# A hybrid mixer layer on one core: the first branch's projection as seven block products, and one late scan head fewer

## The chip, the core and the metric

One core of a Trainium2 chip runs the whole layer. The metric is device time in microseconds of one execution; lower is better. The core has TensorE (PE, matmuls, whose weight loads the profile calls PEld), VectorE (DVE), ScalarE (ACT), GpSimd (POOL) and SyncE (SP). All transfers that matter here are issued from SP's one queue, in its order.

## The reference

```python
px = hx @ w_in + b_in                      # hx: normed, modulated x, 2048 tokens x 1024
u = c_a * x_a
conv = dwconv3(u, w_conv, b_conv)          # along rows of 64 tokens
y_a = b_a * conv * silu(z_a)               # first branch
h = mLSTM forward + backward, 8 heads, chunkwise
y_b = sigmoid(o) * headnorm(h) * silu(z_b) # second branch
merged = sigmoid(g_a) * (y_a @ w_pa) + sigmoid(g_b) * (y_b @ w_pb)
out = rmsnorm(x + gate * (merged @ w_out + b_out))
```

The projections w_pa, w_pb and w_out are 1024 x 1024; w_in has about 11 such blocks of columns. All data is float32.

## The kernel before

**Precision.** A float32 operand is split into a high part (a cast on ACT to the fast format, `split`, L178) and a low part (a subtraction on DVE, L179). A product is three passes: high x high, high x low, low x high. In the trace `wh` and `wl` are the parts of a weight tile, and `x` names both parts of an operand in the 28 slots of the pool xp.

**Halves and stages.** The 2048 tokens are two halves of 1024. The stages run in this order: input products of half 0; of half 1; then four branch stages, each one projection of one half: w_pa of half 1, w_pb of half 1, w_pa of half 0, w_pb of half 0; then the output product with the final norm.

**Two forms of product.** `pair` (matmuls at L427) multiplies two blocks of 128 output columns and both 512-token column blocks of a half in seven block products in place of eight. Product o (0 to 6) takes operand o of `Operands`, a sum or difference of blocks that `combine` wrote to DRAM ahead of time, and weights that `Stream.make` sums on POOL (four sums a pair, L360). A pair is 7 x 4 x 3 = 84 matmuls of 128x512. After the products DVE and ACT add the bank sums together (s1, u2, u3, and `added` at L926). `slab` (matmuls at L474) is the plain form: one block of 128 columns, 8 x 3 matmuls for each of the two token blocks. Before the change the input and output products use pairs, and all four branch stages use slabs on operands loaded by `Branch`.

**Side work.** The state scans, token transposes, gates and preparation of operands are generators that are advanced between matmuls. `run(dense, rate, urate)` takes one step from the queue `later` for every 1/rate matmuls and one from `urgent` for every 1/urate; `flush` runs what is left. PE's order is the order of the code; the other engines' orders come from a scheduler, apart from instructions under `pin`.

**The scan.** The mLSTM runs in chunks of 128 tokens, 8 per head and half. One chunk is 8 steps. It updates the state (PE L658, then DVE L662), takes the scores of the next chunk (PE L834), applies the weights (ACT wt L832, DVE pt L836 and qw L839), multiplies four times into the one PSUM bank pn (L891, L892), divides on DVE (den, rd, L897 to L900) and normalises (ACT hf L904, DVE hb L905). Bank pn is free again after hb. `state_scan` is a shorter form that only carries the state; it too updates through a bank pn. For half 0 the scan of the first EARLY heads runs under the input products of half 1 and the rest, the late heads, under the branch stages; late heads recompute masks on ACT (L816) and POOL (L820). Each finished head of half 0 is loaded and split as an operand of the last branch stage (`yb.fetch`).

## Time and profile before

| | us |
|---|---|
| median of 3 runs | 2660.72 |
| lowest, highest | 2659.01, 2660.84 |
| profiled execution | 2660.47 |
| its span | 2658.7 |
| input products of half 1 end, branch stages begin | 2076.5 |
| last branch stage ends, output begins | 2484.5 |

A row of the profile that groups instructions reads: line, engine, operation, output<-input, shape, count | busy us, mean ns of one | idle time of that engine just before them, and what ended it. A row of a window of time reads: start:end, length, then the busy time of PE, PEld, DVE, ACT and POOL with their counts, the granted PE clock (1 is full), the busy share of the DMA engines, and GB/s. A row of the timeline reads: start, length, engine, line, operation, in square brackets how long the engine had been idle and what ended it. A row of the waits reads: engine, its output, its line <- who was waited for: total us, times, longest.

### The profile page before, as it was taken

What the parts mean: (1) busy time and instruction counts of PE and PEld (TensorE: products, weight loads), DVE (VectorE), ACT (ScalarE), POOL (GpSimd) and SP (SyncE); (2) the same over time, 40 slices, a digit from 0 to 9 for tenths busy, and PEclk for the clock granted to TensorE, in tenths of its full rate; (3) what the DMA queues carried; (4) which work ended last, traced back from release to release, by engine and by line L of the source; (5) the groups of instructions that cost most, each with busy time, mean ns of one, the idle gap of its engine ahead of it and who ended that gap; (6) DMA issues with size and microseconds to landing.
All of it is one profiled execution on the core that took longest, in us unless ns stands there. A gap on an engine that the chain in (4) does not pass through costs nothing.

```text
span 2658.7 us, 38177 instructions
## 1 busy us (share of the span) xinstructions
PE 2594.5 (98%) x12807; PEld 2166.7 (81%) x12807; DVE 1722.6 (65%) x3119; ACT 1099.0 (41%) x2269; POOL 1123.8 (42%) x1322
## 2 busy tenths in 40 slices
PE   8999999999999999999999999999999999999998
PEld 7788887888878787877887888888888888888777
DVE  6643237687776777478578577667666656554597
ACT  5433344333333335344443444344444544442233
POOL 1221223233345553235555555565555124422674
PEclk9999999999999999999999999999999999999999
DMA  8333344655734457435644653653566978768542
GB/s 231 101 101 106 106 139 131 211 167 179 232 118 123 139 145 236 118 100 159 195 142 130 201 160 120 195 174 128 154 195 201 301 219 273 253 194 288 195 159 96
DMA packets 373217, 452.99 MB, mean 170 GB/s; under 512 B 24428, under 2 KB 273948, under 8 KB 373020
## 3 DMA queue, kind: packets, MB, share of 16 engines
q1 hardware_dynamic: 372784, 450.46, 54.4%
q8 instruction: 102, 1.67, 0.3%
q14 instruction: 95, 0.78, 0.1%
q10 hardware_dynamic: 236, 0.08, 0.0%
HBM read 319.42 MB, written 131.03 MB: 169 GB/s over the span
## 4 chain that ended last, share of the span: by engine, by line
PE 48%; DVE 3%; DMA 2%; issue 1%; POOL 1%; ACT 0%; SPq 0%; DVEq 0%; POOLq 0%; ACTq 0%
PE pd L427 29%; PE pd L474 11%; PE pn L891 2%; PE pn L892 2%; PE pa L834 1%; PE pu L658 1%; DMA mgd<-t2k 1%; DVE wl L179 1%; PE pa L849 1%; PE pn L658 0%; PE pa L669 0%; DVE xt L1596 0%; DVE xt L1605 0%; DMA x<-wod 0%; DVE cv L999 0%
## 5 line engine op out<-in xcount | busy, mean ns | idle before, releaser
L427 PE MATMUL pd<-x,wh 128*128 128x512 f32 x5320 | 1695.9, 397 | 15.9 <-DVE xt L1605 8.5
L427 PEld LDWEIGHTS pd<-x,wh 128*128 128x128 f32 x5320 | 985.1, 189 | 209.9 <-issue 19.4
L427 PE MATMUL pd<-x,wl 128*128 128x512 f32 x2660 | 1057.3, 397 | 0.0
L427 PEld LDWEIGHTS pd<-x,wl 128*128 128x128 f32 x2660 | 501.8, 189 | 99.3 <-issue 0.2
L178 ACT CAST wh<-sw 128x512 fp32r<-128x512 f32 x382 | 237.0, 620 | 492.9 <-PE pd L427 409.0
L179 DVE TENSOR_TENSOR wl<-sw,wh 128x512 fp32r<-128x512 f32 x382 | 303.2, 795 | 182.0 <-ACT wh L178 177.1
L178 ACT CAST wh<-wr 128x512 fp32r<-128x512 f32 x350 | 216.6, 619 | 375.3 <-PE pd L427 269.9
L360 POOL TENSOR_TENSOR sw<-wr,sw 128x512 f32<-128x512 f32 x95 | 136.1, 1433 | 432.6 <-DVE wl L179 345.2
L179 DVE TENSOR_TENSOR wl<-wr,wh 128x512 fp32r<-128x512 f32 x350 | 289.7, 828 | 42.5 <-ACT wh L178 39.1
L474 PE MATMUL pd<-x,wh 128*128 128x512 f32 x896 | 281.7, 396 | 0.0
L360 POOL TENSOR_TENSOR sw<-wr 128x512 f32<-128x512 f32 x95 | 130.9, 1378 | 236.9 <-DVE wl L179 236.0
L653 POOL TENSOR_SCALAR vw<-tk,wk 128x129 f32<-128x129 f32 x205 | 161.9, 794 | 120.2 <-PE pn L658 109.7
L474 PEld LDWEIGHTS pd<-x,wh 128*128 128x128 f32 x896 | 166.3, 188 | 32.1
L474 PE MATMUL pd<-x,wl 128*128 128x512 f32 x448 | 173.4, 397 | 0.0
L186 POOL TENSOR_SCALAR ssq<-ssq 128x1 f32<-128x1 f32 x128 | 37.2, 291 | 293.7 <-ACT hf L906 289.8
L926 DVE TENSOR_TENSOR t2k<-pd,u 128x512 f32<-128x512 f32 x168 | 115.5, 688 | 59.8 <-PE pd L427 59.1
L360 POOL TENSOR_TENSOR sw<-sw,wr 128x512 f32<-128x512 f32 x94 | 132.4, 1408 | 47.9 <-DVE wl L179 37.4
L904 ACT ACTIVATE hf<-pn,rd 128x128 f32<-128x128 f32 x128 | 47.0, 367 | 246.9 <-DVE rd L900 222.4
L360 POOL TENSOR_TENSOR sw<-wr,wr 128x512 f32<-128x512 f32 x94 | 132.2, 1406 | 20.2 <-DVE wl L179 10.8
L820 POOL TENSOR_SCALAR_AFFINE_SELECT mw<-mw 128x256 f32<-128x256 f32 x128 | 61.7, 503 | 119.5 <-DMA mw<-mwd 89.1
L891 PE MATMUL pn<-tk,pt 128*128 128x129 f32 x512 | 98.8, 275 | 5.0 <-DVE hb L905 5.0
L891 PEld LDWEIGHTS pn<-tk,pt 128*128 128x128 f32 x512 | 86.8, 190 | 16.2 <-issue 5.8
(259 smaller groups left out, 3317.5 us busy)
## 6 DMA issues: line engine op xcount, KB each, us to landing
wr<-in_w_in_dram SPq DMA_DIRECT2D x176, 512.0 KB, 4.1
tk<-tokd SPq DMA_DIRECT2D x64, 386.0 KB, 3.6
mw<-mwd SPq DMA_DIRECT2D x44, 512.0 KB, 5.3
qkd<-t2k SPq DMA_DIRECT2D x64, 256.0 KB, 2.9
qk<-qkd SPq DMA_DIRECT2D x64, 256.0 KB, 3.8
tk<-tokd SPq DMA_DIRECT2D x48, 257.0 KB, 2.9
tokd<-t2k SPq DMA_DIRECT2D x32, 258.0 KB, 2.9
x<-in_w_ada_dram SPq DMA_DIRECT2D x16, 512.0 KB, 6.4
```

The lines of the kernel that those rows point to most:

```text
L178: a = nc.scalar.copy(hi, raw)
L179: b = (eng or nc.vector).tensor_tensor(lo, raw, hi.bitcast(F32), op=OP.subtract)
L186: nc.gpsimd.tensor_scalar(dst, ss, 1.0 / n, EPS, op0=OP.mult, op1=OP.add)
L360: nc.gpsimd.tensor_tensor(s, a, b, op=op)
L427: nc.tensor.matmul(ps[b], op[wi][:, kk, :], xs.at(o, xi, kk), start=(fresh and kk + pi == 0), stop=(o == last[b] and kk == 3 and pi == 2), ...
L474: nc.tensor.matmul(pss[j], ops[k // 4][wi][:, k % 4, :], y(xi, k, j), start=(k + pi == 0), stop=(k == NK - 1 and pi == 2))
L653: pin(nc.gpsimd.tensor_scalar(vw, tk[:, VT], wk, None, op0=OP.mult))
L820: pin(nc.gpsimd.affine_select(mws[m][:, :, 0, d, :], mws[m][:, :, 0, d, :], pattern=[[0, 2], [s, P]], base=0, channel_multiplier=-s, compa ...
L891: nc.tensor.matmul(pn[:, d, :], pt[:, d, :], tk[:, VT], start=True, stop=False)
L892: nc.tensor.matmul(pn[:, d, :], qw[:, d, :], cur if d == carried else tk[:, ST], start=False, stop=True)
L904: nc.scalar.activation(hf, pn[:, 0, 0:P], AF.Copy, scale=rd[:, 0:1])
L926: nc.vector.tensor_tensor(t, ps, add, op=OP.add)
```

## The change

The first branch's projection is computed in pairs for both halves, by a new class `Gated`. Its operands come from `yad`, which is now laid out in blocks, and `combine` makes the four differences it needs once the last input pair of the first branch (B3) is through: for half 0 with the big tiles it had, for half 1 (`tile` None) with four 512-wide tiles of the pool cv at a time. The half-0 projection now runs straight after half 0's own input products, ahead of half 1's; its result waits in `mad`, which now has a buffer for each half. The order of stages becomes: input half 0, w_pa half 0, input half 1, w_pa half 1, w_pb half 1, w_pb half 0, output. EARLY goes from 3 to 4, so four heads are late where five were: under w_pa half 1 (rate 0.22) and w_pb half 1 (rate 0.55) in place of three branch stages at 0.305. `arriving` loads and splits the operands of w_pb half 1 during the last pair of w_pa half 1. No flush has a step of the scans left in either version. PE has 11200 rows for 11296.

```diff
-    def combine(src, tile):
+    def combine(src, tile=None):
...
-            if kk < 4:
+            if kk < 4 and tile is None:
+                bs[kk] = [vslot() for _ in range(4)]
+                for n, t in enumerate(bs[kk]):
+                    ld.dma_start(t, src[n, :, kk, :])
+            elif kk < 4:
...
-    yad = scratch("yad", [NK, P, T])
+    yad = scratch("yad", [8, P, 4, NB])
...
-    mad = dp.tile([NK, P, T], F32, name="mad")
+    mad = scratch("mad", [NK, P, T])
...
-                ld.dma_start(yad[half][n, :, S2[j]], v)
+                ld.dma_start(yad[half][2 * (n // 4) + j, :, n % 4, :], v)
...
+    class Gated:
+        def __init__(self, half):
+            self.half = half
+            self.tiles = [(2 * p + i, j) for p in range(4) for i, j in ((0, 0), (1, 1), (1, 0), (0, 1))]
+            self.s = deque()
+        def load(self):
+            if self.tiles:
+                n, j = self.tiles.pop(0)
+                s = vslot()
+                ld.dma_start(s, sad[self.half][n, :, S2[j]])
+                self.s.append(s)
+        def begin(self):
+            self.st = Stream((w_pa, 2 * p * P, True) for p in range(4))
+            self.st.begin()
+            self.y = Operands()
+            self.y.load(yad[self.half], range(7))
+            for _ in range(3):
+                self.load()
+        def pairs(self):
+            for p in range(4):
+                def fin(i, j, ps, add):
+                    s = self.s.popleft()
+                    nc.vector.scalar_tensor_tensor(s, s, 1.0, added(ps, add), op0=OP.add, op1=OP.mult)
+                    ld.dma_start(mad[self.half][2 * p + i, :, S2[j]], s)
+                    self.load()
+                yield pair(self.st, self.y, fin)
...
-        run(pair(st, xA, fin), 0.235, 0.5)
+        run(pair(st, xA, fin), 0.212, 0.5)
+        if w == "B3":
+            urgent.append(combine(yad[0], big))
+    flush(urgent)
+    pa = Gated(0)
+    pa.begin()
+    for dense in pa.pairs():
+        run(dense, 0.212, 0.5)
...
-    EARLY = 3
+    EARLY = 4
...
-        run(pair(st, xB, fin), 0.8 if w in ("q0", "o0", "z0") else 0.34, 0.5)
+        run(pair(st, xB, fin), 0.8 if w in ("q0", "o0", "z0") else 0.358, 0.5)
...
+        if w == "B3":
+            urgent.append(combine(yad[1]))
...
-    run(branch(w_pa, ya, PaEnd, 1), RATE, URATE)
...
-    run(branch(w_pb, yb, PbEnd, 1), RATE, URATE)
...
+    pa = Gated(1)
+    pa.begin()
+    ya = Branch(0, lambda k: ybd[1][k], ())
+    def arriving():
+        yield from gap(1)
+        fs = [ya.fetch(k, 1) for k in range(NK)]
+        for o in range(6):
+            yield from gap(12)
+            for k in (2 * o, 2 * o + 1):
+                if o < 4:
+                    next(fs[k])
+            for k in (2 * o - 4, 2 * o - 3):
+                if o > 1:
+                    next(fs[k], None)
+    for p, dense in enumerate(pa.pairs()):
+        if p == 3:
+            urgent.append(arriving())
+        run(dense, 0.22, 1.0)
...
-    run(branch(w_pa, ya, PaEnd, 0), RATE, 0.5)
+    run(branch(w_pb, ya, PbEnd, 1), 0.55, 0.5)
```

In the new file pairs are at L440, slabs at L487, state updates at L671 and L675, den, rd and hb at L910 to L918, `added` at L939, Gated's product at L1081, pt and qw at L849 and L852.

**First place: DVE at the change from the first branch to the second, half 1.** In the kernel before, ahead of and at the start of the second branch (the weight splits wl of its first blocks, scan instructions, the end product L1502 of the first branch):

```order
L897 SCALAR_TENSOR_TENSOR den_22007<-pn_21992,em_129 128x2
L898 TENSOR_TENSOR den_22007<-pn_21992,den_22007 128x2
L900 RECIPROCAL rd_22010<-den_22007 128x2
L905 SCALAR_TENSOR_TENSOR hb_21812<-pn_21992,rd_22010,hf_22012 128x128
L1502 SCALAR_TENSOR_TENSOR t2k_21946<-t2k_21946,pd_21948 128x512
L179 TENSOR_TENSOR wl_22040<-wr_22027,wh_22039 128x512
L662 SCALAR_TENSOR_TENSOR cst_22070<-cst_21964,dec_10588,pu_22071 128x129
```

In the changed kernel, at the same place, the last rows ahead of den_23077, the first division term whose pn is computed in the second branch (x_5739 and x_5741 are low parts of its operands 6 and 7):

```order
L1081 SCALAR_TENSOR_TENSOR cv_22768<-cv_22768,t2k_23003 128x512
L939 TENSOR_TENSOR t2k_23023<-pd_22917,u_22819 128x512
L179 TENSOR_TENSOR wl_23036<-wr_23027,wh_23035 128x512
L1081 SCALAR_TENSOR_TENSOR cv_22884<-cv_22884,t2k_23023 128x512
L179 TENSOR_TENSOR wl_23040<-wr_23033,wh_23039 128x512
L849 SCALAR_TENSOR_TENSOR pt_22990<-pa_22988,wt_22985 128x256
L852 SCALAR_TENSOR_TENSOR qw_22992<-qk_22749,mw_22751 128x256
L179 TENSOR_TENSOR wl_23046<-wr_23033,wh_23045 128x512
L179 TENSOR_TENSOR x_5739_22921<-x_5739_22921,x_5738_22920 128x1024
L179 TENSOR_TENSOR x_5741_22924<-x_5741_22924,x_5740_22923 128x1024
L910 SCALAR_TENSOR_TENSOR den_23077<-pn_23064,em_129 128x2
```

The end work of a pair and the splits of the new operands now stand ahead of a chunk's division, where one product and one weight split stood.

**Second place: DVE at the end of half 0's input products.** In the kernel before, while half 1's operands are loaded (x names their low parts, L662 is a state update):

```order
L179 TENSOR_TENSOR x_2211_9550<-x_2211_9550,x_2209_9548 128x1024
L662 SCALAR_TENSOR_TENSOR tk_9358<-tk_9358,dec_1466,pn_9473 128x129
L441 TENSOR_TENSOR u_9481<-pd_9461,u_9428 128x512
L662 SCALAR_TENSOR_TENSOR cst_9488<-tk_9358,dec_1466,pn_9489 128x129
L179 TENSOR_TENSOR x_2214_9553<-x_2214_9553,x_2212_9551 128x1024
L179 TENSOR_TENSOR wl_9627<-wr_9622,wh_9626 128x512
L926 TENSOR_TENSOR t2k_9502<-pd_9483,u_9481 128x512
L179 TENSOR_TENSOR x_2215_9554<-x_2215_9554,x_2213_9552 128x1024
L179 TENSOR_TENSOR x_2218_9557<-x_2218_9557,x_2216_9555 128x1024
```

In the changed kernel, while the operands of w_pa half 0 are loaded, at about the same operands:

```order
L179 TENSOR_TENSOR x_2153_9418<-x_2153_9418,x_2151_9416 128x1024
L675 SCALAR_TENSOR_TENSOR tk_9233<-tk_9233,dec_1467,pn_9348 128x129
L179 TENSOR_TENSOR wl_9488<-wr_9407,wh_9487 128x512
L939 TENSOR_TENSOR t2k_9354<-pd_9332,u_9330 128x512
L179 TENSOR_TENSOR wl_9498<-sw_9495,wh_9497 128x512
L179 TENSOR_TENSOR x_2156_9421<-x_2156_9421,x_2154_9419 128x1024
L675 SCALAR_TENSOR_TENSOR cst_9366<-tk_9233,dec_1467,pn_9367 128x129
L939 TENSOR_TENSOR t2k_9377<-pd_9358,u_9330 128x512
L763 COPY tk_9285<-cst_9287 128x129
L179 TENSOR_TENSOR x_2157_9422<-x_2157_9422,x_2155_9420 128x1024
L179 TENSOR_TENSOR wl_9502<-wr_9409,wh_9501 128x512
L675 SCALAR_TENSOR_TENSOR tk_9285<-tk_9285,dec_1467,pn_9397 128x129
```

State updates now go on between the operand splits to the last of them; before, they ended in the middle of the load.

**Third place: PE at the start of the last branch stage (w_pb half 0).** In the kernel before, the last transposes of the scan (L849) and the last matmuls of the stage ahead (bank pd_24317), up to the new stage's first:

```order
L849 MATMUL pa_24336<-ident,hb_23850 128x128 x4
L474 MATMUL pd_24317<-x_5650_22823,wh_24146 128x512
L474 MATMUL pd_24317<-x_5651_22824,wh_24146 128x512
L474 MATMUL pd_24317<-x_5650_22823,wl_24147 128x512
L474 MATMUL pd_24317<-x_5680_22957,wh_24146 128x512
L474 MATMUL pd_24317<-x_5681_22958,wh_24146 128x512
L474 MATMUL pd_24317<-x_5680_22957,wl_24147 128x512
L474 MATMUL pd_24399<-x_5767_23306,wh_24371 128x512
```

In the changed kernel (transposes at L862, the stage ahead in bank pd_24606):

```order
L487 MATMUL pd_24606<-x_5740_22923,wh_24327 128x512
L487 MATMUL pd_24606<-x_5741_22924,wh_24327 128x512
L487 MATMUL pd_24606<-x_5740_22923,wl_24328 128x512
L862 MATMUL pa_24648<-ident,hb_24285 128x128 x4
L487 MATMUL pd_24706<-x_5774_23061,wh_24678 128x512
```

The transposes of the last head stood six matmuls ahead of the new stage and now stand at its first.

34 lines of the change are left out of this document (13 added, 21 removed).

## The prediction

> **What bounds the kernel now.** I read the page's engine table first, then busy time by stage, then what TensorE (PE) waits for in each stage, then the distance between its matmuls.
>
> ```profile
> span 2658.7 us, 38177 instructions
> PE 2594.5 (98%) x12807; PEld 2166.7 (81%) x12807; DVE 1722.6 (65%) x3119; ACT 1099.0 (41%) x2269; POOL 1123.8 (42%) x1322
> core 0: us, PE busy (x) PEld busy (x) DVE busy (x) ACT busy (x) POOL busy (x), PEclk, DMA share, GB/s
> 553.00:1042.00 489.00, 476.96 (x2157) 391.25 (x2157) 361.96 (x552) 188.65 (x292) 212.87 (x189) 0.99 0.53 162
> 1042.00:2076.50 1034.50, 1020.21 (x5150) 854.42 (x5150) 707.28 (x1473) 454.67 (x1006) 537.00 (x682) 1.00 0.54 163
> 2076.50:2485.20 408.70, 408.70 (x2050) 345.43 (x2049) 211.78 (x453) 161.93 (x419) 141.21 (x200) 1.00 0.78 249
> ```
>
> The rows of the stages are: the later part of the first half's input products, the second half's, and the four branch stages (first branch half 1, second branch half 1, first branch half 0, second branch half 0). PE is busy without a break in the branch stages, and nothing else there is near its limit. So a matmul that leaves comes off the end at its full distance to the next one. That distance is read where only large matmuls run:
>
> ```profile
> 2396.25 40.71 PE pd L474 x180
> 1217.97 8.41 PE pd L427 x37
> ```
>
> 40.71/180 = 0.226 us for a branch matmul, 8.41/37 = 0.227 for one of a pair. The 397 ns that the groups show for one is its whole pipelined passage, not its price.
>
> **What goes.** A branch takes 8 blocks x 2 halves x 8 x 3 passes = 384 matmuls, the seven-product form 4 pairs x 7 x 4 x 3 = 336. Two of the four branches change: 96 matmuls of 128x512 fewer, and PE's order has exactly 96 rows fewer, 11200 for 11296. 96 x 0.2262 = **21.7 us**. The scan's PE work stays the same, since a head moves and none is dropped. The rest of this part is what is given back, by places.
>
> **Two loads of seven operands in the first half, where one was.** The old change from the first half to the second is such a load, and it cost time:
>
> ```profile
> PE pn L658 <- DVE tk L662: 6.2, 4, 3.0
> 1033.10 0.67 PE L658 MATMUL pn<-vw,tk 128*128 128x129 f32 x2 [2.96 <-DVE tk L662]
> 1030.48 2.22 DVE L179 TENSOR_TENSOR x<-x,x 128x1024 fp32r<-128x1024 f32 x1
> 1034.81 1.04 ACT L178 CAST x<-x 128x1024 fp32r<-128x1024 f32 x1 [2.90 <-DMA x<-xod]
> 1030.00:1035.00 5.00, 2.04 (x7) 1.65 (x7) 4.67 (x7) 2.10 (x4) 1.27 (x1) 0.82 0.97 247
> 1035.00:1040.00 5.00, 5.00 (x20) 4.05 (x19) 3.87 (x6) 3.47 (x5) 0.00 (x0) 0.84 0.87 255
> ```
>
> A state update on PE waited 2.96 us for DVE, which worked on operand splits that came late from the DMA queue, and after it the granted clock was 0.82 and 0.84 over two slices of 5 us: (0.18 + 0.16) x 5 = 1.7 us. That load cost 4.7 us. There the scan was on its last updates; in the changed order the updates go on through the whole first load, each behind a split in DVE's order (front, second place), and the second load meets the last two updates only. I take 4.7 for the first and half of it, 2.4, for the second: net **+2.4** against the 4.7 that go. Bounds: -4.7 (neither waits) to +9.4 (the first meets three such waits, 14.1, the second none).
>
> The Trainium skill (TensorE: Matmul & The Clock Gate, "What's actually happening") says that the clock falls to half after an idle window of about 3.4 us and comes back after as long a busy one. By that page each wait that fills a window would add 3.4/2 = 1.7 us (an estimate from the page) and a shorter one nothing; the row's wait was shorter than the page's window and paid 1.7 all the same, so the trace agrees in the size and not in the limit. With the limit the new waits, taken shorter than it, would pay nothing, and the sum below would be 1.7 + 0.85 = 2.6 us lower, 2646.1.
>
> **Second half into the first branch.** Seven operands of 1 MB take the place of eight of 0.5 MB while the last input pair runs. The old load at this place ran the DMA queue full without a wait:
>
> ```profile
> 2065.00:2070.00 5.00, 5.00 (x25) 3.99 (x24) 4.75 (x8) 4.94 (x9) 2.98 (x3) 1.00 1.01 374
> ```
>
> The late scan starts only after its first eleven steps, 50 matmuls at 0.22, so few instructions couple PE to the splits. Bounds 0 (this row) to 4.7 (the row of the first half); it is nearer to this row's place: **0**.
>
> **First branch into the second, half 1.** Here eight operands are split while the last pair runs, and the scan's rate jumps from 0.22 to 0.55 steps a matmul. In DVE's order (front, first place), from the add that reads the last pair's product 4 to the first division term after the hand-over (den_23077) stand, with the mean durations of these rows and 0.69 for the adds and gate products (L1502's form):
>
> ```profile
> L179 DVE TENSOR_TENSOR x<-x,x 128x1024 fp32r<-128x1024 f32 x30 | 38.5, 1286 | 17.3 <-ACT x L178 16.9
> L179 DVE TENSOR_TENSOR wl<-wr,wh 128x512 fp32r<-128x512 f32 x65 | 50.3, 775 | 29.6 <-ACT wh L178 26.9 <-DMA t2k<-sbd 2.3
> L1502 DVE SCALAR_TENSOR_TENSOR t2k<-t2k,pd 128x512 f32<-128x512 f32 x32 | 21.8, 685 | 18.9 <-PE pd L474 16.7 <-DMA cv<-ybd 1.2 <-DMA qk<-qkd 0.8
> L839 DVE SCALAR_TENSOR_TENSOR qw<-qk,mw 128x256 f32<-128x256 f32 x40 | 17.1, 428 | 0.0
> L836 DVE SCALAR_TENSOR_TENSOR pt<-pa,wt 128x256 f32<-128x256 f32 x40 | 16.9, 423 | 29.0 <-ACT wt L832 26.1 <-PE pd L474 2.0 <-PE pa L834 1.0
> L905 DVE SCALAR_TENSOR_TENSOR hb<-pn,rd,hf 128x128 f32<-128x128 f32 x40 | 14.0, 351 | 20.6 <-ACT hf L904 20.6
> ```
>
> six adds and products (4.1), four operand splits (5.1), four weight splits (3.1), pt, qw and hb (1.2), small ones (0.5): 14.0 us, which can't begin before product 4 ends, 24 matmuls (5.4 us) ahead of the hand-over. So den_23077 comes at about +8.6, and its chain to hb frees bank pn some 1.4 us later, at +10.0. PE gets to the next use of pn after 17 large matmuls (3.9) and one and a half scan steps' small ones (about 1.4): +5.3. Wait 4.7 us; because neighbouring DVE instructions overlap a little (two products of 0.69 take 1.28 in the rows below), some 0.7 us in all, I take **+4.0**. Bounds: 0 (the old hand-overs had no wait) to 9.3 (4.7, a DMA wait of 2.9 as above, and the clock's 1.7).
>
> That DVE doesn't pass a waiting instruction shows in a row of before, where L898 follows L897 in the data and ran 2.8 us later, behind others' work:
>
> ```profile
> 2196.68 0.16 DVE L897 SCALAR_TENSOR_TENSOR den<-pn,em 128x2 f32<-128x2 f32 x1 [1.92 <-PE pn L892]
> 2196.91 1.28 DVE L1518 SCALAR_TENSOR_TENSOR t2k<-t2k,pd 128x512 f32<-128x512 f32 x2
> 2198.11 1.41 DVE L179 TENSOR_TENSOR wl<-wr,wh 128x512 fp32r<-128x512 f32 x1
> 2199.45 0.15 DVE L898 TENSOR_TENSOR den<-pn,den 128x2 f32<-128x2 f32 x1
> ```
>
> **Late scan at 0.55.** Branch stages minus their matmuls: 408.7 - 1536 x 0.2262 = 61.3 us for the 40 late chunks, 1.53 us of PE each. A chunk is 8 steps: at 0.305 that is 26.2 matmuls, 7.5 us a chunk with its own work; at 0.55 it is 14.5, 4.8 us. About 24 chunks fall there. ACT carries most:
>
> ```profile
> L832 ACT ACTIVATE wt<-mw,a 128x128 f32<-128x128 f32 x80 | 29.2, 395 | 18.3 <-POOL mw L820 18.3
> L816 ACT ACTIVATE mw<-mw,mp 128x128 f32<-128x128 f32 x80 | 25.4, 387 | 0.0
> L904 ACT ACTIVATE hf<-pn,rd 128x128 f32<-128x128 f32 x40 | 14.7, 368 | 101.7 <-DVE rd L900 93.8 <-PE pd L474 7.9
> L651 ACT ACTIVATE vw<-tk,wk 128x129 f32<-128x129 f32 x35 | 13.7, 390 | 0.0
> L906 ACT ACTIVATE hf<-hb 128x128 f32<-128x128 f32 x40 | 12.4, 310 | 14.1 <-DVE hb L905 14.1
> L178 ACT CAST wh<-wr 128x512 fp32r<-128x512 f32 x63 | 38.8, 616 | 80.1 <-PE pd L474 79.7
> L178 ACT CAST x<-x 128x1024 fp32r<-128x1024 f32 x29 | 30.3, 1044 | 27.7 <-DMA x<-wod 24.6 <-DMA x<-ybd 2.6 <-DMA x<-yad 0.5
> ```
>
> The first five make 95.4/40 = 2.4 us a chunk, casts (8 of 1.04, 16 of 0.62) another 0.8: 3.2 of 4.8, to which come waits for POOL's masks (18.3/40 = 0.5) and for hb (14.1/40 = 0.4). It fits with 0.7 to spare, and a split or a late DMA uses that up at times. Bounds 0 to 24 x 1.0 (the rival below); nearer to the rows: **+2.0**.
>
> **Smaller places.** The last head's transposes move from six matmuls ahead of the last stage to its very start (front, third place), 1.4 us later. The operand they feed:
>
> ```profile
> 2405.31 1.28 DVE L179 TENSOR_TENSOR cv<-cv,cv 128x512 fp32r<-128x512 f32 x2
> 2407.01 1.07 PE L474 MATMUL pd<-cv,wh 128*128 128x512 f32 x4
> ```
>
> Its low part is ready at 2406.6 and used from the third of these matmuls, 2407.5: 0.9 us to spare, so **+0.5** (0 to 2). In the second half one more early head joins 88 chunks, and sixteen subtractions: waits there sum to 14 us (1034.5 - 1020.2), a tenth more is **+1.0** (0 to 4). The eight new pairs also need 32 weight sums on POOL:
>
> ```profile
> L360 POOL TENSOR_TENSOR sw<-wr,wr 128x512 f32<-128x512 f32 x94 | 132.2, 1406 | 20.2 <-DVE wl L179 10.8 <-issue 2.4 <-DMA wr<-in_w_in_dram 1.0
> ```
>
> Four a pair are 5.6 us of 19 and lie under its matmuls, as in the pairs so far; uncovered they would cost 1.4 each.
>
> **Sum.** The profiled execution took 2660.5 us, 1.8 more than its span, and the median is 2660.7. 2660.5 - 21.7 + 2.4 + 0 + 4.0 + 2.0 + 0.5 + 1.0 = **2648.7**.
>
> **Rivals.** (1) All is hidden, the two loads wait no more than the one did, and only the matmuls show: 2660.5 - 21.7 = 2638.8, to 2642 with small waits. For it: no wait in 408.7 us of branch stages. Against: the 2.96 us at 1033, in a place that now comes twice. (2) Slower: in the second branch of half 1 the chunk stops overlapping with the next and its chain decides. In series: ACT 3.2, masks 0.5, hb 0.4, and from pn's matmuls (about 0.9) to rd another 0.7 are 5.7, against 4.8: it decides from 4.8 on, and at 5.8 costs 24 us over the rest without the 2.0: 2648.7 - 2.0 + 24 = 2671. For it: the jump of the rate; against: scores, masks and weights of chunk n+1 are issued a chunk ahead. (3) The waits at the hand-overs all take their upper bounds (9.4, 4.7, 9.3): 2648.7 + 7.0 + 4.7 + 5.3 = 2666, no change. That the change doesn't do what it says is excluded by the 96 rows.
>
> **Chances.** Forecast with waits of 3 to 16 us (2642 to 2655) 0.62, rival 1 0.12, rival 2 0.10, between them and toward rival 3 0.16. 0.2% (5.3 us) is about what a measurement of this kernel can tell from no change: faster 0.74, same 0.16, slower 0.10. The range reaches from near rival 1, 2640.5, to 2663 on the way to rival 3.
>
> **What would show it.** PE rows of the first branch gone by 96; waits at pn behind operand splits within 12 us of the hand-over to the second branch of half 1; waits at the state update in the first branch of half 0 with a granted clock under 0.9; few waits later in the second branch. It is wrong if that stage shows waits in every chunk, or if the loads show none.

## The result, and the profile after

The changed kernel takes 2684.29 us (median of 4 runs, 2681.47 to 2688.96); the kernel before takes 2660.47 beside it (median of 4). The ratio is 1.0092, 95% interval 1.0075 to 1.011: slower by 24 us, where 12 us faster was forecast. The profiled execution took 2688.96 us, the slowest of the four; the profile below, and the sums made from it, are of that one.

The page of the changed kernel, its span and its first table:

```profile
span 2687.2 us, 38336 instructions
PE 2593.6 (97%) x12711; PEld 2154.2 (80%) x12711; DVE 1802.6 (67%) x3225; ACT 1118.9 (42%) x2288; POOL 1184.6 (44%) x1361
```

The 96 matmuls are gone from PE's count (12807 to 12711), yet its busy time stays (2594.5 to 2593.6). Some of the matmuls must run slower, then, and the span is 28.5 us longer on top. The windows of the changed kernel by stage show where: input products of half 0, w_pa half 0, the first pair of half 1, the rest of half 1, w_pa half 1, w_pb half 1, w_pb half 0.

```profile
75.00:1022.40 947.40, 937.35 (x4490) 776.46 (x4489) 603.33 (x917) 374.26 (x644) 327.33 (x304) 1.00 0.50 154
1022.40:1120.80 98.40, 88.28 (x384) 71.97 (x383) 69.60 (x112) 34.63 (x49) 42.98 (x37) 0.93 0.78 242
1120.80:1152.40 31.60, 25.26 (x97) 19.78 (x96) 23.80 (x30) 13.91 (x21) 5.47 (x4) 0.84 0.75 224
1152.40:2192.20 1039.80, 1018.11 (x5156) 849.70 (x5155) 720.52 (x1523) 454.47 (x1031) 552.38 (x720) 1.00 0.57 171
2192.20:2281.60 89.40, 88.07 (x430) 73.16 (x429) 69.21 (x126) 45.18 (x102) 33.31 (x39) 1.00 0.75 242
2281.60:2420.50 138.90, 128.77 (x702) 106.81 (x700) 81.94 (x222) 72.69 (x221) 74.80 (x117) 0.99 0.83 261
2420.50:2513.20 92.70, 89.57 (x387) 73.24 (x385) 38.43 (x43) 18.79 (x26) 40.87 (x25) 0.98 0.80 259
```

Length less PE's busy time is idle time: 10.1 us in w_pa half 0 and 10.1 in w_pb half 1, where the branch stages before the change had none. The granted clock of 0.93 and 0.84 in the second and third row takes up to 6.9 and 5.1 us more; what of that does not fall into a wait counts as busy.

To put idle time, a slower clock and small waits into one number, I use a stage's **loss**: its length, from its first large matmul (128x512, of a pair or a slab) to the next stage's, less 0.2262 us for each large matmul and 0.111 for every other one. The output's ends with its last matmul. The second price is read from a row pair of the changed kernel's timeline, where two small matmuls start 0.22 us ahead of the next two:

```profile
2319.33 0.38 PE L904 MATMUL pn<-tk,pt 128*128 128x129 f32 x2
2319.55 0.39 PE L905 MATMUL pn<-tk,qw 128*128 128x129 f32 x2
```

So w_pa half 0, with 336 large and 46 other matmuls, loses 98.4 - 76.0 - 5.1 = 17.3 us. All stages, worked out from the starts of their matmuls in the two profiled executions (84 other matmuls of 128x512 are priced as small ones, which puts 5.1 us into the first half's row and 4.6 into the 42 middle pairs, the same in both kernels):

| loss, us | before | changed |
|---|---|---|
| input products half 0, without the last pair | 42.0 | 30.3 |
| their last pair | 5.0 | 2.8 |
| w_pa half 0: first pair, middle two, last | - | 9.5, 0.6, 7.2 |
| input products half 1: first pair | 1.3 | 11.3 |
| 42 middle pairs | 35.5 | 44.7 |
| last pair | 0.3 | 6.9 |
| w_pa half 1 | 1.2 | 3.1 |
| w_pb half 1 | 1.2 | 17.0 |
| w_pa half 0, late | 1.3 | - |
| w_pb half 0 | 0.2 | 5.9 |
| output | 13.6 | 13.4 |
| sum | 101.7 | 152.7 |

51.0 us more loss, less 21.7 for the matmuls, less 0.8 for a first matmul that came earlier, is 28.5, the difference of the spans. The input products of the first half lose 11.7 less without their last pair; the places that lose more come to 66.5, and the last pair, the late w_pa half 0 and the output lose 3.7 less.

**The load of the second half's operands** is the first of them. What PE waited for in the changed kernel from 1100 to 1170 us:

```profile
PE pd L440 <- DVE t2k L939: 4.5, 1, 4.5
PE pa L682 <- DVE t2k L946: 3.7, 1, 3.7
PE pd L440 <- DVE wl L179: 2.6, 1, 2.6
```

Ahead of the first wait, ACT's timeline and then DVE's and PE's (changed kernel):

```profile
1097.43 0.58 ACT L446 COPY u<-pd 128x512 f32<-128x512 f32 x1
1104.16 1.05 ACT L178 CAST x<-x 128x1024 fp32r<-128x1024 f32 x1 [6.16 <-DMA x<-xod]
1105.12 0.61 ACT L178 CAST wh<-wr 128x512 fp32r<-128x512 f32 x1
```

```profile
1105.25 1.23 DVE L179 TENSOR_TENSOR x<-x,x 128x1024 fp32r<-128x1024 f32 x1 [5.56 <-ACT x L178]
1106.39 0.69 DVE L449 TENSOR_TENSOR u<-pd,u 128x512 f32<-128x512 f32 x1
```

```profile
1110.83 0.39 PE L440 MATMUL pd<-x,wl 128*128 128x512 f32 x1
1115.73 1.19 PE L440 MATMUL pd<-x,wh 128*128 128x512 f32 x2 [4.52 <-DVE t2k L939]
```

The cast of an operand stands in ACT's order ahead of the next weight cast, and waits 6.16 us for its load. The subtraction behind it holds DVE for 5.56 us, and the add u2 (L449), which doesn't need the operand at all, stands behind that. PE waits for these adds some 5 us later. In the kernel before, the first cast at this place waited 1.34 us:

```profile
1022.61 1.05 ACT L178 CAST x<-x 128x1024 fp32r<-128x1024 f32 x1 [1.34 <-DMA x<-xod]
```

**The second branch of half 1** is another. What PE waited for there, from 2290 to 2420 us:

```profile
PE pn L904 <- DVE hb L918: 6.6, 7, 1.6
PE pu L671 <- ACT vw L664: 0.9, 2, 0.7
```

Seven waits at pn lie spread over the stage's some 25 chunks, where the prediction had few behind the first.

### The profile page after: what moved, and what is told of

It reads as the page before. It is cut to its first block, busy times and chain, and to the rows that moved or that the text cites. A ratio compares the mean times of both kernels' runs of the same rounds, so it can differ in the third digit from the quotient of the medians.

```text
span 2687.2 us, 38336 instructions
## 1 busy us (share of the span) xinstructions
PE 2593.6 (97%) x12711; PEld 2154.2 (80%) x12711; DVE 1802.6 (67%) x3225; ACT 1118.9 (42%) x2288; POOL 1184.6 (44%) x1361
## 5 line engine op out<-in xcount | busy, mean ns | idle before, releaser
L440 PE MATMUL pd<-x,wh 128*128 128x512 f32 x5768 | 1863.9, 398 | 16.6 <-DVE xt L1657 8.2
L440 PEld LDWEIGHTS pd<-x,wh 128*128 128x128 f32 x5768 | 1077.9, 189 | 232.3 <-issue 13.8
L440 PE MATMUL pd<-x,wl 128*128 128x512 f32 x2884 | 1145.0, 397 | 3.0 <-DVE wl L179 3.0
L440 PEld LDWEIGHTS pd<-x,wl 128*128 128x128 f32 x2884 | 546.0, 189 | 108.6 <-DVE wl L179 3.9
L178 ACT CAST wh<-sw 128x512 fp32r<-128x512 f32 x414 | 256.3, 619 | 530.4 <-PE pd L440 454.4
L179 DVE TENSOR_TENSOR wl<-sw,wh 128x512 fp32r<-128x512 f32 x414 | 326.6, 790 | 178.6 <-ACT wh L178 174.7
L939 DVE TENSOR_TENSOR t2k<-pd,u 128x512 f32<-128x512 f32 x192 | 131.9, 687 | 72.0 <-PE pd L440 70.8
L373 POOL TENSOR_TENSOR sw<-wr,wr 128x512 f32<-128x512 f32 x102 | 145.9, 1430 | 26.1 <-DMA wr<-in_w_pa_dram 13.6
L487 PE MATMUL pd<-x,wh 128*128 128x512 f32 x448 | 145.3, 403 | 0.0
L179 DVE TENSOR_TENSOR x<-x,x 128x1024 fp32r<-128x1024 f32 x70 | 90.6, 1304 | 45.0 <-ACT x L178 44.7
L833 POOL TENSOR_SCALAR_AFFINE_SELECT mw<-mw 128x256 f32<-128x256 f32 x128 | 60.8, 496 | 130.2 <-DMA mw<-mwd 86.8
L946 DVE SCALAR_TENSOR_TENSOR t2k<-pd,cols,u 128x512 f32<-128x512 f32 x73 | 54.7, 750 | 78.7 <-PE pd L440 76.8
L449 DVE TENSOR_TENSOR u<-pd,u 128x512 f32<-128x512 f32 x103 | 70.8, 687 | 52.4 <-PE pd L440 51.0
```

The costliest lines, as they stand in the source:

```text
L178: a = nc.scalar.copy(hi, raw)
L179: b = (eng or nc.vector).tensor_tensor(lo, raw, hi.bitcast(F32), op=OP.subtract)
L373: nc.gpsimd.tensor_tensor(s, a, b, op=op)
L440: nc.tensor.matmul(ps[b], op[wi][:, kk, :], xs.at(o, xi, kk), start=(fresh and kk + pi == 0), stop=(o == last[b] and kk == 3 and pi == 2), ...
L449: nc.vector.tensor_tensor(u2, ps["Y"], s1, op=OP.add)
L487: nc.tensor.matmul(pss[j], ops[k // 4][wi][:, k % 4, :], y(xi, k, j), start=(k + pi == 0), stop=(k == NK - 1 and pi == 2))
```

## Experiments

Ratios are to the kernel before on the same chip, where its median was 2660.6 to 2663.2 us. Line numbers in these kernels lie a little behind those of the changed one.

### The load of the second half's operands

```diff
-                    ld.dma_start(mad[self.half][2 * p + i, :, S2[j]], s)
+                    kept.append((mad[self.half][2 * p + i, :, S2[j]], s))
+                    if self.half or p < 3:
+                        ld.dma_start(*kept.pop())
...
     xB.load(xod, range(7))
+    for d, s in kept:
+        ld.dma_start(d, s)
```

> Only the place of four stores changes: the last four stores to mad of the first half are issued behind the fourteen loads of the second half's operands, instead of between them. Theory S (queue order): in the changed kernel each of these stores waits on SP for VectorE, and the loads behind it go out late; then the loss around this hand-over (7.2 us in the last pair of w_pa half 0 and 11.3 us in the first pair of the second half, together 18.5) falls to 8 to 10 and the time to 2674 to 2677 us. Theory C (place of the casts): the first cast of an operand stands on ScalarE ahead of the weight casts and waits 6.2 us for its load, whatever the stores do; then the first wait of TensorE there (4.5 us) stays, the loss stays above 15, and the time is 2681 us or more.

Measured: 2682.15 us (1.0069, 1.0045 to 1.0094); the two pairs lose 8.4 and 8.7, together 17.1 for 18.5, and a wait of 5.5 us for an add stays. Theory S falls, and the three signs of theory C hold: SP's order does not cost 8 us here. Whether it costs anything can't be told: in the five kernels of the next two sections, which change nothing up to this place, the two pairs lose 14.5 to 17.6.

The next kernel leaves the stores where they are and puts the splits later (`cut` is the split of one operand):

```diff
+    def arriving_x():
+        yield from gap(1)
+        for o in range(7):
+            yield from gap(6)
+            if o > 2:
+                cut(o - 3)
+            yield from gap(6)
+            xB.claim([o])
+            for q in range(2):
+                ld.dma_start(xB.t[o][1][q].bitcast(F32), xod[xB.PLACE[o], :, 2 * q:2 * q + 2, :])
...
+        if p == 3:
+            urgent.append(arriving_x())
+        run(dense, 0.212, 0.5 if p < 3 else 1.0)
```

> The fourteen loads of the second half's operands are issued as each operand of w_pa half 0 comes free, as now, but each operand's cast and subtraction are put three products (36 matmuls, 8.1 us) behind its load. The stores to mad stay between the loads. Theory C (casts placed too early): ScalarE and VectorE no longer wait in front of the weight casts; the loss around the hand-over falls from 18.5 us to 5 or less and the time to 2669 to 2673 us. Theory S (queue order): the loads still stand behind the stores, and the waits only move into the first pair of the second half; the loss stays above 12 and the time above 2678 us.

Measured: 2675.61 us (1.0055, 1.0036 to 1.0073); the pairs lose 1.0 and 7.7, together 8.7. Theory C has the direction, but not the whole: 8.7 is left where the unchanged code loses 14.5 to 18.5 in six executions (16.6 on the mean), so the late splits are worth about 8 us. ACT's timeline of this kernel shows what is left:

```profile
1101.99 1.05 ACT L178 CAST x<-x 128x1024 fp32r<-128x1024 f32 x1
1103.92 1.05 ACT L178 CAST x<-x 128x1024 fp32r<-128x1024 f32 x1 [0.88 <-DMA x<-xod]
1105.29 1.05 ACT L178 CAST x<-x 128x1024 fp32r<-128x1024 f32 x1 [0.32 <-DMA x<-xod]
1106.59 1.06 ACT L178 CAST x<-x 128x1024 fp32r<-128x1024 f32 x1 [0.25 <-DMA x<-xod]
1108.52 1.06 ACT L178 CAST x<-x 128x1024 fp32r<-128x1024 f32 x1 [0.86 <-DMA x<-xod]
1109.48 0.61 ACT L178 CAST wh<-wr 128x512 fp32r<-128x512 f32 x1
```

The 6 us wait is gone. But five operand casts still stand ahead of the next pair's first weight cast, and PE waits 3.7 us for that weight's low part. The same at the load before it, for w_pa half 0 (one generator for both, called in the last input pair too):

```diff
+        if w == "b3":
+            pa = Gated(0)
+            pa.y = Operands(())
+            flush(urgent)
+            urgent.append(arrival(pa.y, yad[0]))
```

> As the kernel with late splits, and the same for the operands of w_pa half 0: their loads go out as each operand of the last input products comes free, casts and subtractions three products behind their loads. Theory C: the loss in the first pair of w_pa half 0 (9.5 us in the changed kernel, 7.4 with late splits at the next hand-over) falls to 2 or less, and the time to 2667 to 2671 us. Rival U: the wait there is the chain of the state updates, which the splits only touch; it keeps over 6 us, and the time is 2674 to 2677.

Measured: 2674.33 us (1.0050, 1.0038 to 1.0062); the first pair of w_pa half 0 keeps 10.4. Rival U holds (unchanged, that pair loses 7.3 to 9.5): the waits there belong to the chain of state updates, as these rows of 1020 to 1052 us show:

```profile
PE pn L671 <- POOL vw L666: 3.7, 2, 2.4
PE pn L671 <- DVE tk L675: 2.8, 1, 2.8
```

### The late scan

```diff
-        run(dense, 0.22, 1.0)
+        run(dense, 0.4, 1.0)
...
-    run(branch(w_pb, ya, PbEnd, 1), 0.55, 0.5)
+    run(branch(w_pb, ya, PbEnd, 1), 0.395, 0.5)
```

> The late scan's steps are spread evenly: 0.40 per matmul in w_pa half 1 (0.22 before) and 0.395 in w_pb half 1 (0.55 before), the same 283 steps in all. Theory R (the rate): in w_pb half 1 the chain of a chunk has 6.7 us again instead of 4.8, the loss there falls from 17.0 us to 4 or less, w_pa half 1 rises from 3.1 to at most 6, and the time falls to 2673 to 2676 us. Rival H (the hand-over and the slabs): the waits in w_pb half 1 come from the operands that arrive and from the slabs, not from the rate; it keeps over 12 us and the time stays above 2681 us.

Measured: 2679.75 us (1.0066, 1.0044 to 1.0088). w_pb half 1 falls from 17.0 to 5.5 (4.3 of it in its first block of columns, 1.2 in the other seven); w_pa half 1 rises from 3.1 to 12.0. The rate is the cause in w_pb half 1, as theory R says, though the time lies between the two theories: w_pa half 1 pays for 0.40 with 3.5 and 3.7 us in its first and last pair, where operands arrive, and 1.9 and 2.9 in the two between.

The next kernel leaves part of the computation out, as its expectation says:

```diff
-                later.append(scan(sp_, [r], 0))
+                later.append(scan(sp_, [r], 0) if r < 3 else empty([r], 36))
...
-    later.append(scan(sp_, range(EARLY, NH), 0, lambda h: heads_done(h), True))
+    later.append(empty(range(EARLY, NH), 35, lambda h: heads_done(h)))
```

> The changed kernel with part of the computation left out: the first half's scan of head 3 within the second half's input products, and the whole late scan (heads 4 to 7 of the first half). Empty steps, the same number, and stores of zeros stand in their places, so the other work keeps its place. Theory L (the scan's own chains cost the time): the second half's input products lose about 36 us behind their first pair, as before the change, instead of 51.6; w_pa half 1 loses 1 or less instead of 3.1; w_pb half 1 loses 4 to 5, all in its first slab, instead of 17.0; w_pb half 0 keeps its 5.9. Time about 2655 us. Rival T (transfers: the operands that arrive, the new combination of the second half's blocks): the second half keeps over 46 and w_pb half 1 over 12, and the time stays above 2673 us.

Measured: 2594.97 us (one execution). The expected time forgot the scans' own 510 matmuls (56.6 us). The losses: w_pa half 1 1.2, w_pb half 1 0.2, w_pb half 0 0.2; the second half's middle pairs 44.2, its last 1.1. Windows of the two w_pb stages of this kernel:

```profile
2247.70:2334.70 87.00, 87.00 (x385) 72.06 (x384) 43.12 (x48) 19.15 (x27) 25.56 (x21) 1.00 0.86 275
2334.70:2421.80 87.10, 87.10 (x386) 72.11 (x385) 40.04 (x42) 18.30 (x26) 42.15 (x25) 1.00 0.74 241
```

With the same operands arriving and no scan, PE is busy without a break at a DMA share of 0.86. So all that w_pb half 1 lost more than before, 15.8 us, and all 5.7 of w_pb half 0 hang on the scan; the hand-over costs nothing by itself. In the second half, head 3 costs the 5.8 us of the last pair and nothing before it, which neither theory said.

Where in a chunk the time goes was tried with the gaps moved:

```diff
-            yield from gap(4)
+            yield from gap(6 if late else 4)
             pt, qw, _ = sp.pop(n)
...
-            yield from gap(3 if late and n % 2 == 0 else 4)
+            yield from gap((1 if n % 2 == 0 else 2) if late else 4)
```

> The changed kernel, with the eight steps of a late chunk divided otherwise: six instead of four ahead of the matmuls into pn, two (one in every second chunk) instead of four (three) behind them. The chain from one chunk's pn over den, rd, hf and hb to the next chunk's pn has then two steps more. Theory P (this chain, in its half of the chunk, is late at 0.55 steps per matmul): w_pb half 1 loses 9 us or less instead of 17.0, and the time falls by 7 to 10 us. Rival W (the whole chunk is too long for 4.8 us, whatever its parts): w_pb half 1 keeps 14 us or more and the time stays within 3 us.

Measured: 2688.24 us (1.0110, 1.0093 to 1.0127), and w_pb half 1 loses 24.9. Theory P falls: the part from pn to hb got two steps more, and the loss rose. It rose by 8 us, and the time by 4, so rival W has the loss and not the time. Those two steps were taken from the other part of the chunk, and the shift the other way was not run; so it is not excluded that this other part is the late one. DVE's waits in that stage, 2290 to 2430 us of this kernel and then 2290 to 2420 of the changed one:

```profile
DVE pt L849 <- ACT wt L845: 28.7, 20, 3.3
DVE den L910 <- PE pn L905: 13.0, 8, 3.1
```

```profile
DVE pt L849 <- ACT wt L845: 20.1, 18, 3.0
DVE den L910 <- PE pn L905: 11.6, 8, 2.5
```

### The second half

```diff
-        run(pair(st, xB, fin), 0.8 if w in ("q0", "o0", "z0") else 0.358, 0.5)
+        run(pair(st, xB, fin), 0.8 if w in ("q0", "o0", "z0") else 0.372, 0.5)
```

> The rate of the scans in the second half's input products is 0.372 steps per matmul instead of 0.358, so that the last chunks end about two pairs before the second half does. Theory E (the end is uncovered): the 6.9 us lost in the last pair of the second half, where the last block of a head is finished with nothing left to put between, fall to under 2, and the time falls by 4 to 6 us, to 2678 to 2681. Rival M (more steps per matmul cost as much elsewhere): the gain at the end is given back in the pairs before, the second half's loss stays between 58 and 66 us beside 62.9 now, and the time is within 2 us of 2684.

Measured: 2685.47 us (1.0084, 1.0064 to 1.0104). The last pair falls from 6.9 to 0.1 as theory E says, but the middle pairs rise from 44.7 to 49.3 and w_pa half 1 from 3.1 to 6.3. Rival M holds for the time.

The next leaves out part of the computation, as its expectation says:

```diff
-            urgent.append(combine(yad[1]))
+            z = t2k()
+            nc.gpsimd.memset(z, 0.0)
+            for kk in range(4):
+                for n in range(4):
+                    ld.dma_start(yad[1][4 + n, :, kk, :], z)
```

> The changed kernel with part of the computation left out: the four block differences of the second half (16 loads, 16 subtractions, 16 stores behind their results) are replaced by 16 stores of zeros that wait for nothing. Theory K (the combination holds SP's queue, and scan loads stand behind it): the 42 middle pairs of the second half lose 35 to 38 us, as before the change (35.5), instead of 44.7. Rival Q (the rate of 0.358 instead of 0.34 steps per matmul): they keep 42 or more.

Measured: 2692.46 us (one execution); the middle pairs lose 53.6. It decides neither theory, because the stores, all issued at once, make a wait of their own: one pair loses 12.2 us (2.6 in the changed kernel). What PE waited for there, from 1985 to 2025 us, and SP's timeline:

```profile
PE pn L905 <- DMA cst<-std: 9.3, 1, 9.3
```

```profile
1995.93 10.09 SPq L1508 DMA_DIRECT2D yad<-t2k  x14
```

Fourteen stores hold SP's queue for 10 us, and the scan's load of its state (cst) is issued behind them, at 2007.56. That is theory K's mechanism, made larger than the combination has it. The other eight of pairs 34 to 42 lose 5.6 together (8.2 in the changed kernel); pairs 1 to 33, where nothing was changed, 35.8 for 33.9. What the combination costs is shown by the kernels below.

### Blocks, or the move?

```diff
+    yc = Branch(1, lambda k: ya0[k], ())
+    urgent.extend(yc.fetch(k) for k in range(NK))
+    run(branch(w_pb, ya, PbEnd, 1), 0.325, 0.3)
...
+    run(branch(w_pa, yc, PaEnd, 0), 0.325, 0.5)
...
-    wo = Operands(())
+    wo = Operands((), 16)
```

> Only the second half's w_pa in seven block products (48 dense matmuls fewer, -10.9 us); the first half's w_pa stays in slabs between w_pb half 1 and w_pb half 0, five late heads at 0.325 steps per matmul over three stages. The last output operands lie in other buffers. Theory V (the moved products took cover from the scans): first half and second half lose what they lost before the change (47 and 37 us, the second half 2 to 4 more for the combination), w_pa half 1 4 to 6, w_pb half 1 5, w_pa half 0 1 to 2, w_pb half 0 at most 2: time 2658 to 2663 us. Rival B (blocks cost it wherever they stand, by their hand-overs): w_pa half 1 and w_pb half 1 lose together over 16, and the time is over 2668 us.

```diff
+    urgent.append(ahead())
+    run(branch(w_pb, ya, PbEnd, 1), 0.345, 0.3)
+    flush(urgent)
+    pa = Gated(0)
+    pa.begin(y0)
...
+        if p == 0:
+            urgent.append(behind())
+        if p == 3:
+            flush(urgent)
+            urgent.append(arriving0())
+        run(dense, 0.345, 1.0)
```

> Both halves' w_pa in seven block products, but the first half's in its old place, between w_pb half 1 and w_pb half 0; five late heads at 0.345 steps per matmul. Theory V: the first and the second half lose 47 and 39 to 41 us, and of the 21.7 us that 96 matmuls are worth, 3 are left after hand-overs (into w_pb half 1 4.5, into w_pa half 0 4, into w_pb half 0 5) and the block products at that rate (2 per pair of blocks in eight pairs above what they lose now): 2655 to 2664 us, 20 us or more under the changed kernel. Rival B (the blocks and their hand-overs, not the move): within 8 us of the changed kernel, over 2676 us.

Measured: 2677.98 us (1.0062, 1.0050 to 1.0074) and 2689.85 (1.0095, 1.0080 to 1.0110). With both halves in blocks and nothing moved the kernel is as slow as the changed one: theory V falls, and leaving w_pa half 0 in its old place saves nothing. There the losses lie elsewhere: 17.1 us in w_pa half 0, 11.8 in w_pa half 1, 25.1 in pairs 34 to the last of the second half. With half 1 alone, the first half loses 44.7 us as the theory said, but the second 54.0 and w_pa half 1 10.7. Its time is rival B's, but w_pa half 1 and w_pb half 1 together lose 14.2, under the rival's 16, so a good part lies in the second half. Both kernels have the rate of 0.34 of before in the second half; pairs 1 to 33 there lose 29.6 and 31.2 (before 29.6, changed 33.9), pairs 34 to 42, where the combination runs, 16.7 and 19.3 (before 5.9, changed 10.8). In the half-1 kernel, DVE from 1890 to 1960 us, and PE behind it:

```profile
DVE cv L303 <- DMA cv<-yad: 4.2, 3, 3.2
DVE cv L303 <- issue: 2.0, 1, 2.0
DVE cv L303 <- DMA yad<-cv: 1.9, 1, 1.9
```

```profile
1919.17 0.46 PE L672 MATMUL pn<-vw,tm 128*128 128x129 f32 x2 [3.26 <-DVE tm L676]
```

DVE stands 8.1 us before the combination's subtractions (L303), 6.1 of it for their loads and buffers (for the other 2.0 the profile shows no cause), and state updates (L676) stand behind them: theory C in another place.

### Mended kernels

Longer gaps in the combination, late splits at the load for w_pa half 1, and, in the first of the two, the other mends:

```diff
             if tile is None:
-                yield from gap(8)
+                yield from gap(14)
...
-            yield from gap(2)
+            yield from gap(2 if tile else 8)
...
-            yield from gap(4)
+            yield from gap(4 if tile else 12)
...
+        if w == "b3":
+            flush(urgent)
+            y1 = Operands(())
+            urgent.append(arrival(y1, yad[1]))
```

> The changed kernel with five mends: late splits at all three loads of seven operands, the last four stores of the first half's mad behind the loads, longer gaps in the second half's combination (14, 8 and 12 steps instead of 8, 2 and 4), the late scan at 0.358 steps per matmul in w_pa half 1 and 0.46 in w_pb half 1. If the losses are what the single runs showed: around the load of the second half's operands 18.5 falls to 4 or less, the middle pairs of the second half from 44.7 to 36 to 40, its last pair and the first of w_pa half 1 together from 8.3 to 3, w_pb half 1 from 17.0 to 6, w_pb half 0 from 5.9 to 2; the first pair of w_pa half 0 keeps 9 to 10. Time 2644 to 2652 us, under the kernel before. Rival (the mends only move the stalls): over 2664 us.

> Only the second half's w_pa in blocks, as in the run with blocks for half 1 only, with late splits at their load, longer gaps in the combination and 0.33 steps per matmul in the late stages. If the losses there came from the combination (11 us in two pairs) and from the casts placed too early (5.9 us in the last pair of the second half, 5.6 in the first of w_pa half 1), both go: second half 37 to 40 us instead of 54.0, w_pa half 1 3 to 5 instead of 10.7, time 2650 to 2656 us, under the kernel before. Rival (the mends only move the stalls): over 2664 us.

Measured: 2677.62 us (1.0060, 1.0046 to 1.0073) and 2666.49 (1.0018, 1.0009 to 1.0027). The gaps do what they should: pairs 34 to 42 lose 7.5 instead of 16.7 with half 1 only, and DVE's waits at L303 are gone from its list; the last pair loses 1.1 instead of 5.9. In the first kernel w_pb half 1 falls to 7.4 and w_pb half 0 to 0.2, since the scan ends earlier. But w_pa half 1 loses 16.5 and 12.9, where 3 to 5 were expected of the second, the second half of the second kernel 42.7 for 37 to 40, and the load of the second half's operands in the first kernel 9.5, no less than with late splits alone. By the times the rival holds for both: the mends work where they are put, and a good part moves on.

```diff
-        run(dense, 0.33, 1.0)
+        run(dense, 0.25, 1.0)
...
-    run(branch(w_pb, ya, PbEnd, 1), 0.33, 0.3)
+    run(branch(w_pb, ya, PbEnd, 1), 0.36, 0.3)
...
-    run(branch(w_pa, yc, PaEnd, 0), 0.33, 0.5)
+    run(branch(w_pa, yc, PaEnd, 0), 0.342, 0.5)
```

> As the mended kernel with blocks for half 1 only, but the late scan runs at 0.25 steps per matmul in w_pa half 1 and at 0.36 and 0.342 in the two stages behind it, the same steps in all. Theory R (what w_pa half 1 loses grows with the scan's rate): its 12.9 us fall to 4 or less, w_pb half 1 stays under 6, w_pa half 0 under 3, and the time falls from 2666.5 to 2656 to 2660 us. Rival A (its first and last pair lose it to the arriving operands): it keeps 9 or more, and the time stays over 2663 us.

Measured: 2660.69 us (1.0003, 0.9995 to 1.0012); w_pa half 1 keeps 9.4, of which 4.4 in the first pair and 4.5 in the last. By the loss and its place that is rival A, the two pairs in which operands arrive; the time lies between the two theories. So in these two the scan was slowed to 0.12:

```diff
-        run(dense, 0.25, 1.0)
+        run(dense, (0.12, 0.36, 0.36, 0.12)[p], 1.0)
...
-        for o in range(6):
-            yield from gap(12)
+        for o in range(7):
+            yield from gap(6)
+            for k in (2 * o - 6, 2 * o - 5):
+                if o > 2:
+                    next(fs[k], None)
+            yield from gap(6)
```

> As the run with the slow late scan in w_pa half 1, but 0.12 steps per matmul in its first and last pair of blocks (where operands arrive) and 0.36 in the two between, 0.365 and 0.347 behind, and the operands of w_pb half 1 are split three products behind their loads instead of two. Theory A (scan chunks and arriving operands stand in each other's way on ScalarE and VectorE in those two pairs): its 9.4 us fall to 4 or less, the rest stays, and the time is 2653 to 2657 us against 2660.7. Rival (the stalls only move to the pairs between and to the stages behind): the late stages together keep 12 us or more of their 13.6, and the time stays over 2659.

```diff
+        if w == "b3":
+            xB = Operands(())
+            urgent.append(arrival(xB, xod))
-        run(pair(st, xA, fin), 0.235, 0.5)
+        run(pair(st, xA, fin), 0.235, 1.0 if w == "b3" else 0.5)
```

> As the run before it, and the second half's operands too are loaded as they come free and split three products behind their loads. Theory C (casts placed too early): the last pair of the first half and the first of the second, 6.5 us together, fall to 3, and the time is 2 to 4 us under that of the run before it. Rival: these pairs keep their 6 us, since the updates of the first half's states and the gate weights stand there too.

Measured: 2660.01 us (0.9990, 0.9981 to 0.9999) and 2659.24 (0.9991, 0.9982 to 1.0001). w_pa half 1 loses 6.2 and 7.2; the two pairs at the first half's end 6.7 and 4.7. Both gains are smaller than theory A and theory C expected. In both kernels the first pair of w_pa half 1 holds none of the scan's matmuls and still loses 3.3 and 4.3 us (PE waits 3.0 and 2.4 for ACT's copy u), and the last 2.1; the two between, at 0.36, lose 0.3 to 0.4 each. This is the fastest form found: 0.1% under the kernel before, which is too little to call it faster. Windows of the last kernel for w_pa half 1, w_pb half 1 and the late w_pa half 0:

```profile
2077.90:2172.70 94.80, 91.03 (x442) 75.49 (x441) 74.67 (x136) 55.40 (x124) 42.03 (x47) 0.98 0.77 248
2172.70:2287.00 114.30, 112.56 (x601) 95.95 (x600) 71.11 (x169) 54.81 (x160) 54.81 (x84) 1.00 0.91 285
2287.00:2396.30 109.30, 109.30 (x575) 93.08 (x574) 58.59 (x144) 46.98 (x132) 30.36 (x59) 1.00 0.70 223
```

The late slab stage has no idle time at 0.347 steps per matmul; the block stage keeps 3.8 us, in its first and last pair, beside a clock of 0.98.

## Why the prediction was wrong

- **What goes, -21.7: right.** 96 matmuls fewer, and the losses and spans close with it.
- **Two loads of seven operands, +2.4: wrong, and the largest error.** The failed step is "the second load meets the last two updates only", and with it the price of half the old load's 4.7. The pairs around both loads lose 30.8 us (2.8, 9.5, 7.2, 11.3) where they lost 6.3: +24.5, of which 18.5 lie at the second load. (In the five other kernels with the same code there they lose 25.1 to 27.9, so some 3 to 6 us of this are of the one execution.) It was reckoned by the state updates that it meets, but what it held up were the adds and weight casts of the block products themselves: an operand cast waited 6.16 us for its load, where the old one waited 1.34. Late splits took about 8 us of it away; what the stores' order adds is within the spread. At the first load the mechanism was the one given (PE at the state update, DVE tk, clock under 0.9), and 9.5 + 2.8 = 12.3 lies within its bound of 14.1; the value taken, 4.7, was too low. The largest of its waits:

```profile
1042.59 0.77 PE L671 MATMUL pn<-vw,tk 128*128 128x129 f32 x2 [3.83 <-DVE tk L675]
```

- **First half's scan: not in the sum.** -11.7, with a lower rate there, 0.212 for 0.235: the same number of steps was spread over 336 matmuls more. In every kernel with 0.235 the pairs of the first half but the last lose 38 to 46 us, with 0.212 28 to 31. No run changed this rate alone; the kernels with 0.212 are also those with w_pa half 0 moved.
- **Second half, +1.0: wrong**, "a tenth more". Its middle pairs lose 9.2 more and its last 6.6. The 14 us of which a tenth was taken (1.4, set down as 1.0) are idle time alone; the loss there was 37.1. The first sum splits into 4.3 in pairs 1 to 33 and 4.9 where the combination runs. The 4.3 goes with the rate and with the one early head more, which no run separates: pairs 1 to 33 lose 29.5 to 32.9 in all kernels at 0.34 and 32.7 to 35.8 at 0.358; the last pair's is head 3's scan, which ends without anything behind it (1.1 when left out, 0.1 at a higher rate, which costs it back elsewhere). Sixteen subtractions of 0.69 us were counted as DVE's work, not as places where DVE stands still.
- **Into w_pa half 1, 0:** measured +1.9, near the value taken, in part by luck: in the mended kernels its first and last pair lose 2 to 7 each, the first 3.3 and 4.3 even where none of the scan's matmuls run in it. The row that carried it, a full DMA queue without a wait, came from a load into slabs.
- **Into w_pb half 1, +4.0: right in size, by another way.** Its first block of columns loses 5.6 us, and 4.3 at the lower rate; without the scan nothing. The chain forecast is there: den follows the operand subtractions at 2290.61, 9.1 us behind the hand-over (8.6 forecast). But PE waits only 1.0 us at pn, because it had already waited 2.47 at the state update and then had a clock of 0.66 over 5 us. That first wait comes from the chunk before, whose rd, behind operand subtractions too, was done only at 2280.6: its norm on POOL, the masks behind it in POOL's order (L833), and ACT's wt and vw followed. The sum had no path through POOL (PE, ACT, POOL):

```profile
2287.38 0.49 PE L671 MATMUL pu<-vw,tk 128*128 128x129 f32 x2 [2.47 <-ACT vw L664]
2292.21 0.49 PE L904 MATMUL pn<-tk,pt 128*128 128x129 f32 x2 [1.00 <-DVE hb L918]
```

```profile
2286.27 0.76 ACT L845 ACTIVATE wt<-mw,a 128x128 f32<-128x128 f32 x2 [2.60 <-POOL mw L833]
```

```profile
2282.59 1.92 POOL L186 TENSOR_SCALAR ssq<-ssq 128x1 f32<-128x1 f32 x1 [15.76 <-ACT hf L919]
```

- **Late scan at 0.55, +2.0: the mechanism of rival 2, mis-sized.** The other seven blocks lose 11.4 us, and 1.2 at 0.395. "It fits with 0.7 to spare" summed ACT's instructions and two waits; rival 2 had the chain and a price of 24, twice the measured one. PE waits in some chunks only, so the whole chain does not decide every one. From one chunk's first matmul into pn to the next's it is 5.3 us on the mean of these blocks, where the sum had 4.8 and rival 2 5.8. That the part from pn to hb alone is late is refuted; which link is, stays open.
- **Last head, +0.5:** measured 5.7. The sum had looked at the operand's low part, from DVE; PE waits for the high part, a cast on ACT, and the clock drops behind it (changed kernel, timeline and window):

```profile
2433.15 0.51 PE L487 MATMUL pd<-cv,wh 128*128 128x512 f32 x1 [2.87 <-ACT cv L178]
```

```profile
2435.00:2440.00 5.00, 5.00 (x17) 3.93 (x17) 2.61 (x3) 0.62 (x1) 2.99 (x2) 0.70 0.79 265
```

It loses 0.2 without the scan, and 0.2 when the scan ends earlier (the first mended kernel, whose rates have room for 296 steps where the scan takes 283): the last head was late by more than the 1.4 us read from the order.

The sum closes: -21.7 + 24.5 + 0.6 (the middle of w_pa half 0) - 11.7 + 9.2 + 6.6 + 1.9 + 15.8 + 5.7 - 0.2 = 30.7, less the 1.3 us of the late w_pa half 0 that is gone and 0.8 of the start: 28.6, for a measured 28.5.

The Trainium skill's rule on the clock (TensorE: Matmul & The Clock Gate, "What's actually happening"), half speed after an idle window of about 3.4 us, stands as it did in the prediction: the wait of 4.5 us, longer than that, was followed by half clock (0.50 in the last section), and so was the wait of 2.87 us, which was shorter (0.70 over the window of 5 us shown above). By the Trainium skill's limit the second would have cost nothing behind it.

Not taken apart, so that the cause stays open: the 8.7 us that late splits leave at the second half's load, the 10.4 at w_pa half 0, and the 6 to 7 that w_pa half 1 keeps in the best form.

## What to carry to other kernels

Price a hand-over by the instructions that stand behind an operand's cast or subtraction on their engines' orders, not by the load or by the arithmetic: casts placed ahead of landings that came later cost about 8 us at one place, as much as 35 of the 96 saved matmuls. A form with fewer matmuls per stage also has less room for the side work, and the room has to be counted per stage before the matmuls are. The blocks themselves took the scan as slabs do (0.3 to 0.4 us a pair at 0.36 steps per matmul); what kept costing were the pairs in which the next operands arrive. Spread a loaded step's load, arithmetic and store by the landing times seen in the trace.

## What was not expected of the hardware

After a wait of PE the granted clock was half for a while. The changed kernel's windows around the second load:

```profile
1110.00:1115.00 5.00, 1.21 (x6) 0.67 (x4) 5.00 (x7) 3.39 (x5) 2.18 (x1) 0.86 0.86 220
1115.00:1120.00 5.00, 4.27 (x10) 3.47 (x11) 3.28 (x5) 1.44 (x2) 0.00 (x0) 0.50 0.82 290
1120.00:1125.00 5.00, 4.13 (x17) 3.00 (x16) 5.00 (x7) 4.59 (x7) 0.00 (x0) 0.95 0.80 239
```

The first 0.73 us of the second window still belong to the wait of 4.52. In the other 4.27 us ten matmuls start where 19 fit at full clock: 9 x 0.2262 = 2.0 us on top of the wait. Shorter waits do the same or nothing. The first of these windows (changed kernel) holds the end of a wait of 1.80 us, the second (kernel before) a whole wait of 2.91, and the 5 us behind it are at 1.00 too:

```profile
1290.00:1295.00 5.00, 4.57 (x15) 3.80 (x16) 4.29 (x10) 1.16 (x3) 1.11 (x2) 0.66 0.38 104
1850.00:1855.00 5.00, 2.09 (x15) 1.58 (x13) 4.77 (x9) 1.98 (x6) 4.92 (x5) 1.00 0.00 0
```

At the first one's place in the code the kernel with the stores behind the loads waited 1.79 us and kept a clock of 1.00. So the same wait can cost (1 - 0.66) x 5 = 1.7 us more in one execution than in another.

The second surprise is that transfers alone cost nothing (w_pb half 1 without the scan, a DMA share of 0.86, no idle time), while fourteen stores ahead of one small load cost a wait of 9.3 us.
